# Attention queries of a two-layer model on one core: the rotated parts of four heads in one block of rows, the rest two heads to a block

## The chip, the cores and the metric

The kernel runs on one core of one Trainium2 chip. The metric is the device time of one execution in microseconds; a quoted time is the median of several runs. The profile is of one further execution, and its times are counted from the first instruction of the span.

## The reference, cut to what matters

A model of two layers works on 256 tokens `x` and 256 context tokens `ctx` of width 1024. Layer 0 mixes tokens by an attention of 8 heads beside a long convolution of 512 channels; layer 1 by a gated linear attention; each layer ends in a feed-forward part with a convolution of width 3. All weights are float32. What the change touches is the query of layer 0: 96 numbers for each head, 64 of them plain and 32 rotated (only for the tokens of `x`, not for the context).

```python
q = (rmsnorm(z[..., :256], q_norm_g) @ w_q_b).reshape(lead + (8, 64 + 32))      # for x and for ctx
kv = (rmsnorm(z[..., 256:384], kv_norm_g) @ w_kv_b).reshape(lead + (8, 64 + 64))
q = concatenate([q[..., :64], axial_rope(q[..., 64:], cos, sin)], axis=-1)       # tokens of x only
k, v = keys_values(kv, axial_rope(k_rope, cos, sin))                             # one k_rope for all heads
o = softmax(q k^T / sqrt(96)) v      # 256 queries of x over 512 keys, 256 queries of ctx over their own 256
```

`axial_rope` multiplies a pair of numbers eight places apart with the cosine and the sine of an angle that depends on the token alone, so it is the same for all heads.

## The kernel before

Activations of both sequences lie side by side, 512 tokens along the free dimension. A float32 product is made by `mm3` from two rounded halves of each factor: three matmuls (lines 191 to 193), high by high, high by low, low by high, with the halves made by a copy on ScalarE (line 185 for large weights) and a subtraction on VectorE (line 186).

The stretch around the change is layer 0's mixer. `self.ORDER` (line 1387) lists in which order its pieces are emitted: the heads `("H", 0)` to `("H", 7)`, the long convolutions `c1` and `c2`, the projections `hy` that feed these, the products of attention weights and values `pv`, and six blocks of the modulation weights of layer 0, `mod`, each of which streams 2 MB through two buffers of 512 KB (`mod_row`, line 257). The list is not the order on the engines: a planner with a simulated time line places every emitted instruction on its engine's queue, so that pieces lie interleaved; on the chip each engine then runs its queue in that order.

A head (`mla_head`, line 752) does this. For an even head `head_weights` (line 739) loads the query and key weights of two heads (two DMAs into `hraw`), copies them to `hwh` on ScalarE and subtracts on GpSimd to get `hwl`. Two inner blocks of 128 times three matmuls give the head's 96 query rows for 512 tokens in a PSUM bank `sc`. ScalarE writes them, scaled, to `q` (line 146, by way of `mul_s`). `rope` (line 670) rotates rows 64 to 95 of `q` for the 256 tokens of `x` in four VectorE instructions: a shuffle of partitions (line 674), two products with the table `rope_t` (lines 675 and 676) and a sum (line 677). An even head also projects the keys of two heads and ScalarE copies them to `kt`. Then, four times, a score matmul (line 780), a row maximum on VectorE (line 782), an exponential on ScalarE (line 784), a scaling by the reciprocal of the sum (line 785 and, by way of `mul_s`, 146 or 147), transposes on TensorE (line 789), and a copy out of PSUM (to `ptx` or `ptc`, line 141). There are two `sc` banks and one `tp` bank for this. `mla_first` (line 698) prepares the normalised `zh`, `zl` for all heads, the rotated key rows, and the values.

The long convolution (`long_conv`, line 618) multiplies spectra in lines 650 to 653, on VectorE or on GpSimd; the sums `ua` of lines 639, 640, 655 and 656 are on VectorE.

Of the kernel before, what the change touches and what calls it, by code (L numbers as in the profile page):

```python
# [9 lines left out]
F32 = mybir.dt.float32  # L10
# [14 lines left out]
def constants():  # L25
    c = {}
    c["ident"] = np.eye(128, dtype=np.float32)


    f = np.arange(128) + 0.5  # L30
    tp = np.arange(128)
    mats = []
    for par in range(2):
        ang = 2.0 * np.pi * np.outer(2 * tp + par, f) / 512.0
        mats += [np.cos(ang), np.sin(ang)]
    for par in range(2):
        ang = 2.0 * np.pi * np.outer(f, 2 * tp + par) / 512.0
        mats += [np.cos(ang) / 256.0, np.sin(ang) / 256.0]
    c["dft"] = np.stack(mats, axis=1).reshape(128, 8 * 128).astype(np.float32)

    order = np.concatenate([np.arange(0, 256, 2), np.arange(1, 256, 2)])
    t = np.linspace(0.0, 1.0, 256, dtype=np.float32)[:, None]
    w = (np.float32(2.0 * math.pi) * np.arange(256, dtype=np.float32)[:, None] / np.float32(256)).astype(np.float32)
    fb = np.linspace(1e-4, 15, 16, dtype=np.float32)
    z = np.concatenate([t, np.cos(fb * w), -np.sin(fb * w)], axis=-1).astype(np.float32)
    c["zfeat"] = np.ascontiguousarray(z[order].T)
    lo, hi = math.log(1e-2) / 1.5, math.log(1e-2) / 0.3
    deltas = np.abs(np.linspace(lo, hi, 512, dtype=np.float32))
    win = np.exp(-t * deltas).astype(np.float32)
    c["win"] = np.ascontiguousarray(win.reshape(128, 2, 512)).reshape(128, 1024)  # L50

    rows = SEQ // 64
    row = np.repeat(np.arange(rows), 64).astype(np.float32)
    col = np.tile(np.arange(64), rows).astype(np.float32)
    inv = (np.float32(10000.0) ** (-np.arange(8, dtype=np.float32) / np.float32(8))).astype(np.float32)
    ang = (np.stack([row, col], axis=-1)[..., None] * inv).astype(np.float32)
    rc = np.zeros((32, SEQ), np.float32)
    rs = np.zeros((32, SEQ), np.float32)
    for ax in range(2):
        for half in range(2):  # L60
            for k in range(8):
                i = ax * 16 + half * 8 + k
                rc[i] = np.cos(ang[:, ax, k])
                rs[i] = np.sin(ang[:, ax, k]) * (-1.0 if half == 0 else 1.0)
    c["rope"] = np.concatenate([rc, rs], axis=1)

    i = np.arange(128) % 32
    m = np.zeros((128, 5, 32), np.float32)
    for lv in range(5):
        blk = i >> lv  # L70
        m[:, lv, :] = (blk[:, None] ^ 1) == blk[None, :32]
    c["mask"] = m.reshape(128, 5 * 32)
    return c
# [9 lines left out]
def host(inputs):  # L83

    src = {n: np.ascontiguousarray(inputs[n]) for n in _INS}
    c = constants()
    cols = np.concatenate([np.asarray(inputs[n]).reshape(-1, 128) for n, _ in COLS]).T
    src["cols0"], src["cols1"] = np.ascontiguousarray(cols[:, :NC0]), np.ascontiguousarray(cols[:, NC0:])
    hyp = np.zeros((64, 386), np.float32)
    hyp[:33, 0:256] = c.pop("zfeat")  # L90
    hyp[:33, 256:320] = inputs["hy_w1"][0]
    hyp[:, 320:384] = inputs["hy_w2"][0]
    hyp[:, 384] = inputs["hy_b1"][0]
    hyp[:, 385] = inputs["hy_b2"][0]
    src["hyp"] = hyp
    src.update(c)
    return src

# [2 lines left out]

ENG = dict(pn=(0, 1, 0, 0), pt=(0, 0, 1, 0), q=1, kv=(1, 1), es=1, uh=0, po=1, pr=2, c1=0, zl=0, zh=2, hwh=1, hwl=2, am=(0, 0), sd=(0, 0), ov=1)


class Kern:
# [562 lines left out]
    def rope(self, pool, v):  # L670

        nc = self.nc
        sh = pool.tile([96, 256], F32, tag="rsh", bufs=1, name="rsh")[64:96, :]
        nc.vector.stream_shuffle(sh, v, [i ^ 8 for i in range(32)])
        nc.vector.tensor_tensor(sh, sh, self.rope_t[64:96, 1, :], op=ALU.mult)
        nc.vector.tensor_tensor(v, v, self.rope_t[64:96, 0, :], op=ALU.mult)
        nc.vector.tensor_tensor(v, v, sh, op=ALU.add)

    def tok(self, t):
# [18 lines left out]
    def mla_first(self, mp, pool):  # L698
# [26 lines left out]
        for i in (1, 2):  # L725
            nc.scalar.copy(self.kt[i][64:96, :], kr)

        r = self.load_raw(A["mla_w_kv_b"][0], 0, 1, 0, 1024)
        kvh, kvl = self.split_w(r)
        ov = self.const.tile([128, 2, 4, 512], F32, tag="xo", bufs=1, name="ov")  # L730
# [7 lines left out]

    def head_weights(self, pool, hp):
        nc, A = self.nc, self.A  # L740
        raw = pool.tile([128, 512], F32, tag="hraw", bufs=1, name="hraw")
        nc.sync.dma_start(out=raw[:, :384].rearrange("p (k n) -> p k n", k=2),
                          in_=A["mla_w_q_b"][0][:, hp * 192 : hp * 192 + 192].rearrange("(k p) n -> p k n", p=128))
        nc.sync.dma_start(out=raw[:, 384:].rearrange("p (h c) -> p h c", h=2),
                          in_=A["mla_w_kv_b"][0][:, hp * 256 : hp * 256 + 256].rearrange("p (h c) -> p h c", h=2)[:, :, :64])
        h = pool.tile([128, 512], F32R, tag="hwh", bufs=1, name="hwh")
        l = pool.tile([128, 512], F32R, tag="hwl", bufs=1, name="hwl")
        self.cp(ENG["hwh"], h, raw)
        self.tt(ENG["hwl"]).tensor_tensor(l, raw, h.bitcast(F32), op=ALU.subtract)
        self.hw = (h, l)  # L750

    def mla_head(self, pool, h):
        nc = self.nc
        if h % 2 == 0:
            self.head_weights(pool, h // 2)
        ps = self.bank("sc")
        qbh, qbl = [w[:, :384].rearrange("p (k n) -> p k n", k=2) for w in self.hw]
        kvh, kvl = [w[:, 384:] for w in self.hw]
        for k in range(2):
            c = slice((h % 2) * 96, (h % 2) * 96 + 96)  # L760
            self.mm3(ps[:96, :], (qbh[:, k, c], qbl[:, k, c]), (self.zh[:, k, :], self.zl[:, k, :]), k == 0, k == 1)
        q = pool.tile([96, 512], F32, tag="q", bufs=2, name="q")
        self.mul_s(ENG["q"], q, ps[:96, :], 1.0 / math.sqrt(96.0))
        self.rope(pool, q[64:96, 0:256])
        if h % 2 == 0:

            ps = self.bank("sc")
            self.mm3(ps, (kvh, kvl), (self.zh[:, 2, :], self.zl[:, 2, :]), True, True)
            for i in range(2):
                self.cp(ENG["kv"][i], self.kt[(h + i) % 3][:64, :], ps[64 * i : 64 * i + 64, :])  # L770
        k = self.kt[h % 3]

        sums = pool.tile([128, 4], F32, tag="sums", bufs=2, name="sums")
        ri = pool.tile([128, 4], F32, tag="ri", bufs=2, name="ri")
        ptx = pool.tile([128, 4, 256], F32, tag="ptx", bufs=self.PT, name="ptx")
        ptc = pool.tile([128, 2, 256], F32, tag="ptc", bufs=self.PT, name="ptc")
        for t in range(4):
            c0, n = (0, 512) if t < 2 else (256, 256)
            sc = self.bank("sc")
            nc.tensor.matmul(sc[:, :n], lhsT=q[:, self.tok(t)], rhs=k[:, c0 : c0 + n], start=True, stop=True)  # L780
            nm = pool.tile([128, 1], F32, tag="nm", bufs=4, name="nm")
            nc.vector.tensor_reduce(nm, sc[:, :n], axis=AX.X, op=ALU.max, negate=True)
            p = pool.tile([128, 512], F32, tag="p", bufs=2, name="p")
            nc.scalar.activation(p[:, :n], sc[:, :n], AF.Exp, bias=nm, accum_out=sums[:, t : t + 1])
            nc.vector.reciprocal(ri[:, t : t + 1], sums[:, t : t + 1])
            self.mul_s(ENG["pn"][t], p[:, :n], p[:, :n], ri[:, t : t + 1])
            tp = self.tpps()
            for j in range(n // 128):
                nc.tensor.transpose(tp[:, j * 128 : j * 128 + 128], p[:, j * 128 : j * 128 + 128], self.ident)
            dst = (ptx if t < 2 else ptc)[:, :, (t % 2) * 128 : (t % 2) * 128 + 128]  # L790
            self.cp(ENG["pt"][t], dst, tp[:, :n].rearrange("p (j c) -> p j c", c=128))
        self.pt[h % 2] = (ptx, ptc)
# [44 lines left out]
    def layer0(self):  # L837
        nc, A, tc = self.nc, self.A, self.tc
        with ExitStack() as lc:
# [3 lines left out]
            with self.banks("start", mm=4, tp=2, sc=2):  # L843
# [28 lines left out]
                second = self.anchors  # L872
                m1x = ExitStack()
                m1 = m1x.enter_context(self.pool("mla1", "right"))
                self.rope_t = sp.tile([96, 2, 256], F32, name="rope_t")
                with self.after([self.mod_dma]):
                    nc.sync.dma_start(out=self.rope_t[64:96].rearrange("p a b -> p (a b)"), in_=A["rope"])
                    nc.sync.dma_start(out=self.colt[:, NC0:], in_=A["cols1"])

                nc.gpsimd.tensor_scalar(self.ones, self.ident, 0.0, 1.0, op0=ALU.mult, op1=ALU.add)  # L880
# [540 lines left out]
```

## Time and profile before

| | |
|---|---|
| median of 3 runs | 1170.69 us (1168.97 to 1174.04) |
| the profiled execution | 1175.04 us |
| its span, first to last instruction | 1173.3 us |
| TensorE busy with matmuls | 1137.6 us, 97% |
| VectorE busy | 861.5 us, 73% |
| ScalarE busy | 519.7 us, 44% |
| GpSimd busy | 276.2 us, 24% |
| DMA queue that SyncE issues, share of 16 engines | 42.7% |

A busy TensorE is not a TensorE at its peak: the record of a matmul lasts until its result has left the array, and matmuls overlap, so that the time from one start to the next is the price of one. The share of busy time is a mean over stages with different limits.

### The profile page before, as it was taken

The page shows a single profiled execution, that of the slowest core. Times are in us where ns is not written, and L with a number is a line of the kernel's source. Part 1 is how long each engine was busy: PE and PEld are TensorE (multiplying, and loading weights), DVE is VectorE, ACT ScalarE, POOL GpSimd, SP SyncE. Part 2 cuts the span into 40 slices and gives each one's busy share as a digit, 9 for nine tenths or more (in the row PEclk, how much of TensorE's full clock was granted, in tenths as well). Part 3 has the DMA queues.
Part 4 walks back from the last instruction along what each step waited for, and adds up shares of the span by engine and source line. Part 5 has one row for each costly group of instructions (what it writes and reads, how often), then busy time and mean ns, then how long its engine had stood idle before and what let it go on. Part 6 is the DMA issues. An engine that isn't in the chain of part 4 may idle for free. (4 is left out here: it accounts for less than half of the span.)

```text
span 1173.3 us, 17955 instructions
## 1 busy us (share of the span) xinstructions
PE 1137.6 (97%) x7094; PEld 928.2 (79%) x7094; DVE 861.5 (73%) x1284; ACT 519.7 (44%) x896; POOL 276.2 (24%) x285
## 2 busy tenths in 40 slices
PE   7999988999999999999999999999999999999997
PEld 3587865445888888888888888888888989999985
DVE  4668897786669997989988447565767766877753
ACT  3554333433245444212444236445465456666542
POOL 3110333341011142100111001535657311111110
PEclk9999999998999999999999999999999999999999
DMA  9543221454135552657764223323223354565550
GB/s 338 189 126 90 81 73 43 148 175 154 64 128 196 181 177 93 207 203 246 257 203 138 90 73 108 108 80 102 73 77 105 109 179 140 183 199 173 171 195 36
DMA packets 118055, 167.57 MB, mean 143 GB/s; under 512 B 4658, under 2 KB 74866, under 8 KB 117908
## 3 DMA queue, kind: packets, MB, share of 16 engines
q1 hardware_dynamic: 117540, 165.38, 42.7%
q8 instruction: 56, 0.92, 0.3%
q10 hardware_dynamic: 432, 1.05, 0.2%
q14 instruction: 27, 0.22, 0.1%
HBM read 165.37 MB, written 1.05 MB: 142 GB/s over the span
## 5 line engine op out<-in xcount | busy, mean ns | idle before, releaser
L186 DVE TENSOR_TENSOR lo<-raw,hi 128x1024 fp32r<-128x1024 f32 (+1 forms) x205 | 262.0, 1282 | 151.0 <-ACT hi L185 146.7
L185 ACT CAST hi<-raw 128x1024 fp32r<-128x1024 f32 (+1 forms) x205 | 213.5, 1047 | 325.0 <-PE mm L192 191.8
L192 PE MATMUL mm<-al,hi 128*128 128x512 f32 (+2 forms) x992 | 340.2, 344 | 1.2 <-DVE al L420 1.0
L191 PE MATMUL mm<-ah,hi 128*128 128x512 f32 (+2 forms) x992 | 339.9, 345 | 1.0 <-DVE ah L419 1.0
L193 PE MATMUL mm<-ah,lo 128*128 128x512 f32 (+2 forms) x992 | 340.1, 344 | 0.0
L192 PEld LDWEIGHTS mm<-al,hi 128*128 128x128 f32 x992 | 188.1, 190 | 23.2 <-DVE al L420 1.5
L191 PEld LDWEIGHTS mm<-ah,hi 128*128 128x128 f32 x992 | 187.5, 190 | 23.8 <-DVE ah L419 1.4
L193 PEld LDWEIGHTS mm<-ah,lo 128*128 128x128 f32 x992 | 188.0, 190 | 22.1 <-issue 0.5
L520 POOL TENSOR_TENSOR y<-y 128x512 f32<-128x512 f32 (+1 forms) x44 | 53.5, 1216 | 377.2 <-DVE y L463 319.4
L308 DVE SCALAR_TENSOR_TENSOR macc<-mraw,cs,macc 128x512 f32<-128x512 f32 x140 | 111.1, 804 | 8.7 <-DMA mraw<-in_mod_w_dram 8.0
L191 PE MATMUL mm<-hi,gh 128*128 128x512 f32 x242 | 94.6, 391 | 0.0
L193 PE MATMUL mm<-hi,gl 128*128 128x512 f32 x242 | 94.3, 390 | 0.0
L192 PE MATMUL mm<-lo,gh 128*128 128x512 f32 x242 | 94.2, 390 | 0.0
L191 PE MATMUL mm<-hi,ah 128*128 128x512 f32 (+1 forms) x192 | 74.7, 389 | 0.3 <-DVE modc L285 0.3
L192 PE MATMUL mm<-lo,ah 128*128 128x512 f32 (+1 forms) x192 | 73.7, 384 | 0.0
L193 PE MATMUL mm<-hi,al 128*128 128x512 f32 (+1 forms) x192 | 73.3, 385 | 0.0
L1159 POOL TENSOR_TENSOR gQ<-gQ,gT 128x256 f32<-128x256 f32 x56 | 54.7, 997 | 47.2 <-PE ga L1129 20.4
L1152 DVE TENSOR_TENSOR gK<-gK,gT 128x512 f32<-128x512 f32 (+1 forms) x56 | 50.6, 948 | 13.6 <-ACT gkc L1105 10.4
L193 PEld LDWEIGHTS mm<-hi,gl 128*128 128x128 f32 x242 | 45.4, 188 | 9.5
L192 PEld LDWEIGHTS mm<-lo,gh 128*128 128x128 f32 x242 | 45.4, 188 | 9.3
L191 PEld LDWEIGHTS mm<-hi,gh 128*128 128x128 f32 x242 | 45.4, 188 | 9.2
L459 ACT ACTIVATE y<-mm,col 128x512 f32<-128x512 f32 (+1 forms) x74 | 50.9, 687 | 2.6 <-DVE gl L522 2.6
(301 smaller groups left out, 1779.4 us busy)
## 6 DMA issues: line engine op xcount, KB each, us to landing
mraw<-in_mod_w_dram SPq DMA_DIRECT2D x96, 512.0 KB, 4.7
raw<-in_ffn_w_up_dram SPq DMA_DIRECT2D x44, 1024.0 KB, 5.6
raw<-in_ffn_w_down_dram SPq DMA_DIRECT2D x20, 1024.0 KB, 5.1
raw<-in_hg_w_in_dram SPq DMA_DIRECT2D x20, 1024.0 KB, 5.0
raw<-in_ab_w_in_dram SPq DMA_DIRECT2D x6, 1024.0 KB, 5.2
raw<-in_ab_w_out_dram SPq DMA_DIRECT2D x4, 1024.0 KB, 5.0
raw<-in_hg_w_out_dram SPq DMA_DIRECT2D x4, 1024.0 KB, 5.0
x<-in_x_dram SPq DMA_DIRECT2D x2, 1024.0 KB, 8.3
```

Of the source, the lines that this page charges most:

```text
L185: nc.scalar.copy(hv, v)
L186: nc.vector.tensor_tensor(lv, v, hv.bitcast(F32), op=ALU.subtract)
L191: mm(ps, lhsT=l[0], rhs=r[0], start=start, stop=False)
L192: mm(ps, lhsT=l[0], rhs=r[1], start=False, stop=False)
L193: return mm(ps, lhsT=l[1], rhs=r[0], start=False, stop=stop)
L308: nc.vector.scalar_tensor_tensor(acc[s], w, c, acc[s], op0=ALU.mult, op1=ALU.add)
L459: nc.scalar.activation(y, ps, AF.Identity, scale=w[1], bias=b)
L520: nc.gpsimd.tensor_tensor(ys[1], ys[0], ys[1], op=ALU.mult)
L1152: nc.vector.tensor_tensor(kv, kv, tv, op=ALU.mult)
L1159: nc.gpsimd.tensor_tensor(qv, qv, tq, op=ALU.mult)
```

## The change

The host reorders the query weights: first the 64 plain columns of all heads (512 columns), then the 32 rotated columns of all heads (256). `mla_first` gets a new block that loads the 256 rotated columns (`qraw`, 256 KB), splits them, projects them once, four heads to a block of 128 rows (two blocks, six matmuls each), scales them on ScalarE into `qr` and rotates each block in one call of `rope` over 128 rows; `rope_t` therefore holds the table four times over (256 KB instead of 64 KB). An even head then projects the plain rows of two heads as one block of 128 rows (six matmuls), and for each of the two ScalarE writes 64 scaled rows to `q` and copies the 32 rotated rows from `qr` below them (`cp` with `ENG["qr"]=1` is ScalarE). An odd head projects nothing. There are three `q` buffers instead of two, and `hraw`, `hwh`, `hwl` have 384 columns instead of 512. `self.ORDER` is the same.

```diff
-    c["rope"] = np.concatenate([rc, rs], axis=1)
+    c["rope"] = np.tile(np.concatenate([rc, rs], axis=1), (4, 1))
...
+    wq = np.asarray(inputs["mla_w_q_b"])[0].reshape(256, 8, 96)
+    src["mla_w_q_b"] = np.concatenate([wq[:, :, :64].reshape(256, 512), wq[:, :, 64:].reshape(256, 256)], axis=1)[None]
...
+QB = 3
+ENG = dict(qr=1, pn=(0, 1, 0, 0), ...
...
     def rope(self, pool, v):
-        sh = pool.tile([96, 256], F32, tag="rsh", bufs=1, name="rsh")[64:96, :]
+        ps = slice(0, 128) if v.shape[0] == 128 else slice(64, 96)
+        sh = pool.tile([128, 256], F32, tag="rsh", bufs=1, name="rsh")[ps, :]
         nc.vector.stream_shuffle(sh, v, [i ^ 8 for i in range(32)])
-        nc.vector.tensor_tensor(sh, sh, self.rope_t[64:96, 1, :], op=ALU.mult)
-        nc.vector.tensor_tensor(v, v, self.rope_t[64:96, 0, :], op=ALU.mult)
+        nc.vector.tensor_tensor(sh, sh, self.rope_t[ps, 1, :], op=ALU.mult)
+        nc.vector.tensor_tensor(v, v, self.rope_t[ps, 0, :], op=ALU.mult)
         nc.vector.tensor_tensor(v, v, sh, op=ALU.add)
...
     def mla_first(self, mp, pool):
...
+        raw = pool.tile([128, 2, 256], F32, name="qraw")
+        nc.sync.dma_start(out=raw, in_=A["mla_w_q_b"][0][:, 512:].rearrange("(k p) n -> p k n", p=128))
+        qrh = pool.tile([128, 2, 256], F32R, name="qrh")
+        qrl = pool.tile([128, 2, 256], F32R, name="qrl")
+        nc.scalar.copy(qrh, raw)
+        nc.vector.tensor_tensor(qrl, raw, qrh.bitcast(F32), op=ALU.subtract)
+        self.qr = mp.tile([128, 2, 512], F32, name="qr")
+        for j in range(2):
+            ps = self.bank("sc")
+            for k in range(2):
+                self.mm3(ps, (qrh[:, k, self.tok(j)], qrl[:, k, self.tok(j)]), (self.zh[:, k, :], self.zl[:, k, :]), k == 0, k == 1)
+            nc.scalar.mul(self.qr[:, j, :], ps, 1.0 / math.sqrt(96.0))
+            self.rope(pool, self.qr[:, j, 0:256])
...
     def head_weights(self, pool, hp):
-        raw = pool.tile([128, 512], F32, tag="hraw", bufs=1, name="hraw")
+        raw = pool.tile([128, 384], F32, tag="hraw", bufs=1, name="hraw")
...
     def mla_head(self, pool, h):
         if h % 2 == 0:
             self.head_weights(pool, h // 2)
-        ps = self.bank("sc")
-        for k in range(2):
-            c = slice((h % 2) * 96, (h % 2) * 96 + 96)
-            self.mm3(ps[:96, :], (qbh[:, k, c], qbl[:, k, c]), (self.zh[:, k, :], self.zl[:, k, :]), k == 0, k == 1)
-        q = pool.tile([96, 512], F32, tag="q", bufs=2, name="q")
-        self.mul_s(ENG["q"], q, ps[:96, :], 1.0 / math.sqrt(96.0))
-        self.rope(pool, q[64:96, 0:256])
-        if h % 2 == 0:
+            ps = self.bank("sc")
+            for k in range(2):
+                self.mm3(ps, (qbh[:, k, :], qbl[:, k, :]), (self.zh[:, k, :], self.zl[:, k, :]), k == 0, k == 1)
+            self.q2 = [pool.tile([96, 512], F32, tag="q", bufs=QB, name="q") for _ in range(2)]
+            for i in range(2):
+                self.mul_s(ENG["q"], self.q2[i][:64, :], ps[64 * i : 64 * i + 64, :], 1.0 / math.sqrt(96.0))
+                j = (h + i) % 4
+                self.cp(ENG["qr"], self.q2[i][64:96, :], self.qr[32 * j : 32 * j + 32, (h + i) // 4, :])
             ps = self.bank("sc")
             self.mm3(ps, (kvh, kvl), (self.zh[:, 2, :], self.zl[:, 2, :]), True, True)
...
+        q = self.q2[h % 2]
...
-                self.rope_t = sp.tile([96, 2, 256], F32, name="rope_t")
+                self.rope_t = sp.tile([128, 2, 256], F32, name="rope_t")
```

## Rows read from the trace of the kernel before

**Rows 1.** Busy time of each engine in stretches of the mixer of layer 0, on the core; behind the stretch its length in us, then for each engine its busy us and, in brackets, its instructions, then the granted TensorE clock as a share of full speed, the DMA engines' share and GB/s.

```profile
76.00:108.00 32.00, 30.31 (x143) 23.91 (x142) 24.92 (x42) 15.08 (x23) 2.80 (x2) 1.00 0.36 106
...
150.00:190.00 40.00, 32.77 (x167) 23.22 (x166) 36.64 (x71) 15.54 (x34) 19.21 (x17) 0.91 0.18 60
...
250.00:290.00 40.00, 35.99 (x176) 18.30 (x174) 26.54 (x55) 12.88 (x26) 11.07 (x12) 0.91 0.48 154
76.00:290.00 214.00, 198.94 (x1002) 133.15 (x1001) 168.78 (x314) 82.08 (x159) 59.08 (x51) 0.97 0.35 110
```

**Rows 2.** Who TensorE's matmuls waited for between 76 and 290 us: us in total, times, longest us.

```profile
PE tp L789 <- DVE p L147: 4.3, 2, 3.6
PE sc L780 <- ACT p L784: 3.8, 3, 2.3
PE tp L789 <- DVE ptx L141: 2.7, 1, 2.7
PE sc L780 <- DVE q L677: 1.4, 1, 1.4
```

**Rows 3.** The matmuls of the query and key projections that read `hwh` (their shapes with their counts at the end), and two of them in the time line of TensorE, one behind the other (start us, us).

```profile
L191 PE MATMUL sc<-zh,hwh x20: 387/396/504, 108.8 to 256.9; 128*96 128x512 f32 x16, 128*128 128x512 f32 x4
...
236.21 0.40 PE L192 MATMUL sc<-zl,hwh 128*96 128x512 f32 x1
236.44 0.39 PE L193 MATMUL sc<-zh,hwl 128*96 128x512 f32 x1
```

**Rows 4.** The rotation of the queries on VectorE, 100 to 285 us, by shape: busy us, mean ns of one, idle time before.

```profile
L676 DVE TENSOR_TENSOR q<-q,rope_t 32x256 f32<-32x256 f32 x8 | 8.4, 1048 | 0.0
L675 DVE TENSOR_TENSOR rsh<-rsh,rope_t 32x256 f32<-32x256 f32 x8 | 4.4, 547 | 0.2
L677 DVE TENSOR_TENSOR q<-q,rsh 32x256 f32<-32x256 f32 x8 | 3.8, 469 | 0.3
L674 DVE STREAM_SHUFFLE rsh<-q 32x256 f32<-32x256 f32 x8 | 3.5, 437 | 0.3
```

**Rows 5.** The time line around 176 us, VectorE, GpSimd and TensorE: start us, us, engine, line, in brackets the idle time before and what ended it.

```profile
175.26 0.69 DVE L141 COPY vx<-cv 128x512 f32<-128x512 f32 x1
176.33 2.57 DVE L676 TENSOR_TENSOR q<-q,rope_t 32x256 f32<-32x256 f32 x1
178.93 0.69 DVE L141 COPY ptx<-tp 128x512 f32<-128x512 f32 x1
176.03 2.58 POOL L921 TENSOR_TENSOR vx<-vx,vx 128x1024 f32<-128x1024 f32 x1 [0.46 <-DVE vx L141]
179.67 0.44 PE L789 MATMUL tp<-ident,p 128*128 128x128 f32 x2 [2.68 <-DVE ptx L141]
```

**Rows 6.** The time line around 260 us, VectorE and TensorE, and the same score matmuls of the head before at 244 us.

```profile
259.82 0.44 DVE L674 STREAM_SHUFFLE rsh<-q 32x256 f32<-32x256 f32 x1
260.71 1.11 DVE L675 TENSOR_TENSOR rsh<-rsh,rope_t 32x256 f32<-32x256 f32 x1
261.74 0.94 DVE L676 TENSOR_TENSOR q<-q,rope_t 32x256 f32<-32x256 f32 x1
264.78 0.66 PE L789 MATMUL tp<-ident,p 128*128 128x128 f32 x2 [3.62 <-DVE p L147]
265.55 3.78 PE L780 MATMUL sc<-kt,q 96*128 96x512 f32 x4
...
244.84 1.88 PE L780 MATMUL sc<-kt,q 96*128 96x512 f32 x4
```

**Rows 7.** The time line around 224 us: the scores that waited for the sum of a rotation (VectorE), and the modulation matmuls behind them.

```profile
223.46 0.42 DVE L677 TENSOR_TENSOR q<-q,rsh 32x256 f32<-32x256 f32 x1
223.93 1.98 PE L780 MATMUL sc<-kt,q 96*128 96x512 f32 x4 [1.44 <-DVE q L677]
227.13 1.05 PE L270 MATMUL mm<-mraw,cs 128*32 128x512 f32 x4 [0.23 <-DMA mraw<-in_mod_w_dram]
```

**Rows 8.** The first of six projection matmuls on TensorE at about 187 us, and the last, the sixth.

```profile
186.69 0.63 PE L192 MATMUL mm<-al,hi 128*128 128x512 f32 x1
...
188.82 0.46 PE L191 MATMUL mm<-ah,hi 128*128 128x512 f32 x1
```

**Rows 9.** The front of the stretch: a product over 128 partitions and 256 columns and a split of weights on VectorE, and one issue of SyncE (start us, us).

```profile
102.89 0.42 DVE L652 TENSOR_TENSOR ut<-ut 128x256 f32<-128x256 f32 x1
...
108.28 1.21 DVE L186 TENSOR_TENSOR lo<-raw,hi 128x1024 fp32r<-128x1024 f32 x1
...
66.82 0.34 SPq L169 DMA_DIRECT2D raw<-in_mla_w_kv_b_dram  x1
```

**Rows 10.** Groups on ScalarE between 76 and 285 us that are nearest to its new work: busy us, mean ns of one, idle time before and what ended it.

```profile
L146 ACT ACTIVATE q<-sc 96x512 f32<-96x512 f32 x8 | 4.7, 592 | 9.7 <-PE sc L193 9.7
L141 ACT COPY kt<-sc 64x512 f32<-64x512 f32 x8 | 4.7, 583 | 6.9 <-PE sc L193 6.9
L726 ACT COPY kt<-kt 32x512 f32<-32x512 f32 x2 | 1.1, 613 | 0.0
```

**Rows 11.** DMA issues: the head weights of the queries (KB each, median us to landing), and the modulation loads on SyncE from 206 us (start, us from the first issue to the last), with the times to landing of their 22 issues.

```profile
hraw<-in_mla_w_q_b_dram SPq DMA_DIRECT2D x4, 192.0 KB, 4.4
...
206.04 73.25 SPq L266 DMA_DIRECT2D mraw<-in_mod_w_dram  x22
...
DMA to landing us min/median/max: 3.6/3.7/5.8
```

More of the change, by code (lines that the diff above doesn't have):

```diff
@@ L100 @@
 GSB = 2
-ENG = dict(pn=(0, 1, 0, 0), pt=(0, 0, 1, 0), q=1, kv=(1, 1), es=1, uh=0, po=1, pr=2, c1=0, zl=0, zh=2, hwh=1, hwl=2, am=(0, 0), sd=(0, 0), ov=1)
+QB = 3
+ENG = dict(qr=1, pn=(0, 1, 0, 0), pt=(0, 0, 1, 0), q=1, kv=(1, 1), es=1, uh=0, po=1, pr=2, c1=0, zl=0, zh=2, hwh=1, hwl=2, am=(0, 0), sd=(0, 0), ov=1)
 class Kern:
@@ L740, in head_weights @@
         nc, A = self.nc, self.A
-        raw = pool.tile([128, 512], F32, tag="hraw", bufs=1, name="hraw")
-        nc.sync.dma_start(out=raw[:, :384].rearrange("p (k n) -> p k n", k=2),
-                          in_=A["mla_w_q_b"][0][:, hp * 192 : hp * 192 + 192].rearrange("(k p) n -> p k n", p=128))
-        nc.sync.dma_start(out=raw[:, 384:].rearrange("p (h c) -> p h c", h=2),
+        raw = pool.tile([128, 384], F32, tag="hraw", bufs=1, name="hraw")
+        nc.sync.dma_start(out=raw[:, :256].rearrange("p (k n) -> p k n", k=2),
+                          in_=A["mla_w_q_b"][0][:, hp * 128 : hp * 128 + 128].rearrange("(k p) n -> p k n", p=128))
+        nc.sync.dma_start(out=raw[:, 256:].rearrange("p (h c) -> p h c", h=2),
                           in_=A["mla_w_kv_b"][0][:, hp * 256 : hp * 256 + 256].rearrange("p (h c) -> p h c", h=2)[:, :, :64])
-        h = pool.tile([128, 512], F32R, tag="hwh", bufs=1, name="hwh")
-        l = pool.tile([128, 512], F32R, tag="hwl", bufs=1, name="hwl")
+        h = pool.tile([128, 384], F32R, tag="hwh", bufs=1, name="hwh")
+        l = pool.tile([128, 384], F32R, tag="hwl", bufs=1, name="hwl")
         self.cp(ENG["hwh"], h, raw)
@@ L755, in mla_head @@
             self.head_weights(pool, h // 2)
-        ps = self.bank("sc")
-        qbh, qbl = [w[:, :384].rearrange("p (k n) -> p k n", k=2) for w in self.hw]
-        kvh, kvl = [w[:, 384:] for w in self.hw]
-        for k in range(2):
-            c = slice((h % 2) * 96, (h % 2) * 96 + 96)
-            self.mm3(ps[:96, :], (qbh[:, k, c], qbl[:, k, c]), (self.zh[:, k, :], self.zl[:, k, :]), k == 0, k == 1)
-        q = pool.tile([96, 512], F32, tag="q", bufs=2, name="q")
-        self.mul_s(ENG["q"], q, ps[:96, :], 1.0 / math.sqrt(96.0))
-        self.rope(pool, q[64:96, 0:256])
-        if h % 2 == 0:
+            qbh, qbl = [w[:, :256].rearrange("p (k n) -> p k n", k=2) for w in self.hw]
+            kvh, kvl = [w[:, 256:] for w in self.hw]
+            ps = self.bank("sc")
[6 more added lines that the diff above has]
+                self.cp(ENG["qr"], self.q2[i][64:96, :], self.qr[32 * j : 32 * j + 32, (h + i) // 4, :])
             ps = self.bank("sc")
@@ L874, in layer0 @@
                 m1 = m1x.enter_context(self.pool("mla1", "right"))
-                self.rope_t = sp.tile([96, 2, 256], F32, name="rope_t")
+                self.rope_t = sp.tile([128, 2, 256], F32, name="rope_t")
                 with self.after([self.mod_dma]):
-                    nc.sync.dma_start(out=self.rope_t[64:96].rearrange("p a b -> p (a b)"), in_=A["rope"])
+                    nc.sync.dma_start(out=self.rope_t.rearrange("p a b -> p (a b)"), in_=A["rope"])
                     nc.sync.dma_start(out=self.colt[:, NC0:], in_=A["cols1"])
```

## The prediction

> **What bounds the kernel now.** The page of the profile has TensorE busy for 97% of the span, so the first question is whether the stretch that the change touches is full as well. The stretches of the mixer answer it [rows 1]: between 76 and 290 us TensorE is busy 199 of 214 us, and of the 15 us that are missing 7.2 lie between 150 and 190 us and 4.0 between 250 and 290 us. In the first of these VectorE is busy 36.6 of 40 us. Both have a granted clock of 0.91: part of the time TensorE ran at 1.2 GHz and not at 2.4. The next view is who TensorE waited for [rows 2]: 4.3 us for a scaled row on VectorE, 3.8 us for exponentials, 2.7 us for a copy out of PSUM on VectorE, 1.4 us for the sum of a rotation. Three of these four are VectorE's queue. So the stretch has two limits: where long matmul blocks lie it is TensorE's work, and between the scores and the products of a head it is a chain in which VectorE comes last. The change takes work from both, and puts some on ScalarE, which is busy 82 of the 214 us.
>
> **TensorE's work.** The query matmuls are 16 for each of three kinds, 48 [rows 3]. After, there are 4 pairs by 6, and 2 blocks by 6 in front: 36. One costs the time to the next start, 0.23 us, not its recorded 0.39 us [rows 3]; a block of 128 weight columns has the same 512 columns to stream, and I take the same. 12 fewer give -2.8 us where TensorE is the limit and 0 where it waits anyway; I take -2.8. The Trainium skill, "TensorE: Matmul & The Clock Gate", section "Back-to-back issue gap", gives about 131 ns as the sustained spacing of matmuls of 512 columns. By it the term would be 12 x 0.131 = -1.6 us; the trace disagrees, with 0.23 us, and the trace decides.
>
> **VectorE's work.** Eight rotations take 8.4 + 4.4 + 3.8 + 3.5 = 20.1 us [rows 4], 2.5 us for a head. Two remain beside the keys' own. Their price over 128 rows is no row of before; the nearest, a product over 128 partitions and 256 columns, took 0.42 us [rows 9], near the 0.47 us that a sum over 32 rows took in the mean [rows 4]; the dearest of the old products took 2.57 us [rows 5]. Time goes by columns, not by rows, so four instructions at 0.42 are 1.7 us for each call. The new split is one subtraction over 512 columns, about half of the 1.21 us of the 1024-column one [rows 9]. So VectorE loses some 16 us in the heads and gains 4.0 us in front of them. What that is worth is read wait by wait.
>
> At 176 us a product of the rotation ran 2.57 us beside a GpSimd product of 2.58 us, where the eight of its kind took 1.05 us in the mean [rows 4, 5]. The copy to `ptx` stood behind it, and TensorE waited 2.68 us for that copy [rows 5]. Without the rotation the copy follows the one that ended at 175.95 us. Next in line is that copy's own 0.69 us, before the wait began; I take the whole wait, -2.7 us, between 0 and that.
>
> At 260 us three instructions of the rotation, 0.44 + 1.11 + 0.94 = 2.5 us, lie ahead of the scaled row for which TensorE waited 3.62 us [rows 6]. What is late next is the same scaled row, behind two small modulation operations. I take -2.5 us, between 0 and -3.6.
>
> At 224 us the scores waited 1.44 us for the sum of the rotation itself. But the second modulation block behind them already waited 0.23 us for its DMA [rows 7], and that landing does not move with the scores. I take half, -0.7, between 0 and -1.4. The 3.8 us behind exponentials [rows 2] hang on row maxima that stand behind convolution products; I take nothing of it, though up to 2.3 could go.
>
> **The clock.** After both long waits TensorE fell to 1.2 GHz. Five matmuls from 186.69 us on are (188.82 - 186.69) / 5 = 0.43 us apart and not 0.23, 1.0 us lost [rows 8], and four scores took 3.78 us where the head before took 1.88, 1.9 us lost [rows 6]. If the waits go, some of the fall goes with them: half, -1.5 us, between 0 and -2.9.
>
> **What it adds.** ScalarE gets eight copies from `qr` to `q` and two scalings of a whole block, and one cast. The nearest rows are 0.59 us for 96 or 64 rows and 0.61 us for 32 rows [rows 10]: price goes by columns, and a quarter of the rows is no cheaper. 11 x 0.6 = 6.6 us more on an engine that is idle 132 of 214 us [rows 1]. For a pair ScalarE now has four writes of queries and two of keys in a run, 3.5 us, where an even head had three, 1.8 us, and an odd one a single write. If exponentials of the head before stand behind it, TensorE waits for its score banks: between 0 and 4 x 1.8 = 7.1 us. I take +1.0, near the free end, because a query written early by two heads has no rotation to wait for and its place in the queue is loose.
>
> In front, 4.0 us of VectorE work join the chain that feeds the third convolution projection, while the first head's own 1.7 us leave it, so its splits (one at 108.28 us, [rows 9]) come up to 2.3 us later. What hides it is the matmuls of the weights split before: TensorE is busy 30.3 of the 32 us up to 108 [rows 1]. If that cover is gone, 2.3 us are lost; I take +1.0.
>
> The query weights are as many bytes as before: 4 loads of 192 KB [rows 11] become 4 of 128 KB and one of 256 KB. The extra load is one issue more on SyncE's queue, emitted ahead of that of the value weights at 66.8 us [rows 9], and with some 4.4 us to landing [rows 11] it is there long before the first query matmul at 108.8 us [rows 3]. The table's 192 KB more pass when no load bounds TensorE. The smaller weight splits on GpSimd and the third `q` buffer only loosen. All of this at 0.
>
> **The sum.** -2.8 - 2.7 - 2.5 - 0.7 - 1.5 + 1.0 + 1.0 = -8.2 us. All pieces are placed anew by the planner, though, and the place where one wait ended is where the next one in line is found; I take back a quarter of the 7.4 us of waits and clock, +1.9. That leaves -6.3 us. The profiled execution took 1175.04 us, so it would take 1168.7; the median of the runs is 4.35 us below that execution, so the median becomes 1164.4, 0.5% faster. About 0.5%, 5.9 us, is also what a measurement of this kernel can tell from no change: a gain counts as one below 1164.8. My own range for this case is 1158 to 1169.
>
> **Rivals.** *The waits go whole.* TensorE's 2.8, the whole of 2.7, 3.6, 1.4 and 2.3 us of waits and 2.9 us of clock, and nothing new: -15.7 us, 1155. For it speaks that VectorE is the last releaser in most waits; against it, that convolution work stands in the same queue.
>
> *The modulation loads set the pace from 206 us on.* 22 loads of 512 KB pass two buffers in 73.25 us, each takes 3.7 us to land [rows 11] and its matmuls about 1.05 us [rows 7]. At two buffers, 11 rounds of 4.75 us, 52 us, is the least. So there are 21 us of room in all, but a single round has little, as at 227 us. Then gains behind 206 us are lost. Ahead of it 30 matmuls become 30 (12 in front and 3 pairs), -2.7 and the first clock loss of 1.0 remain, and the additions of +2.0: about -1.7 us, 1169: no difference.
>
> *ScalarE's run takes the place of the rotation.* If the run of six writes stands ahead of the exponentials in each of the four pairs, TensorE loses 7.1 us, and since the same scores and transposes then wait for ScalarE, none of the waits above is won. With 2.3 us in front and -2.8 of work: +6.6 us, 1177. It decides against the change once the run costs more than some 2.1 us for a pair, with the waits not won. For it: exponentials are what TensorE waits for already, 3.8 us [rows 2]. Against it: ScalarE's idle time. The Trainium skill, "PSUM — Partial Sum Buffer", section "Engine vs sequencer instructions", says that ScalarE's queue is strictly first in, first out. By that rule an exponential cannot pass the run, which is what this rival needs; no run here shows it yet for the new order.
>
> **How the numbers follow.** The forecast has 0.55, with 0.33 of it beyond 0.5% and 0.22 inside; the waits going whole 0.09; the modulation loads 0.15, within 0.5%; ScalarE's run 0.21, of which 0.18 is slower by over 0.5% and 0.03 within. Faster 0.42, same 0.40, slower 0.18. The range goes from a microsecond short of the waits going whole, 1156, to two short of ScalarE's full price, 1175; some 0.06 lies below and 0.14 above.
>
> **What would show it.** In the profile after: 36 query matmuls; two rotations over 128 rows at 0.42 us an instruction; VectorE's busy time between 76 us and the end of the mixer down by 10 to 16 us and ScalarE's up by about 6; no wait for a rotation, and the waits for `ptx` and the scaled row shorter; a granted clock nearer to 1 in both stretches; the first `ab_w_out` matmuls some 6 us earlier, and the distance from there to the end unchanged. It is wrong if TensorE's waits for exponentials grow past 3.8 us, if the modulation matmuls wait for DMA by more than a microsecond or two, or if the part behind the mixer moves.

## The result, and the profile after

The changed kernel takes 1164.55 us, the median of 14 runs (1160.93 to 1171.09); the kernel before took 1170.99 us beside it (14 runs, 1168.97 to 1176.14). The ratio is 0.9944, with a 95% interval of 0.9928 to 0.9961: 6.4 us faster. The forecast was 1164.4.

The two profiled executions differ by more, 1173.3 against 1162.5 us of span, and the difference has to be divided first. Both kernels run the same matmul `mm<-hi,ah` at the start of the stretch (the first block of `ab_w_in`) and at its end (the first block of `ab_w_out`). I call the time between these two the mixer. Before, it goes from 45.48 to 285.50 us, after from 40.86 to 273.40 us. So 4.6 us of the 10.8 lie ahead of it, 7.5 in it, and behind it the changed kernel is 1.3 us longer. The 4.6 us belong to that one execution of the kernel before: eight matmuls at 13.9 us took 7.17 us there and 3.67 us after, by lines that the change does not touch, and a later kernel with the order of the one before (below) came to its mixer at 41.22 us, as all the other profiled executions did between 40.8 and 41.3 us. -7.5 + 1.3 is -6.2, near the 6.4 of the medians.

The whole mixer of the kernel before, with the columns of [rows 1]:

```profile
45.48:285.50 240.02, 224.96 (x1148) 155.46 (x1146) 183.47 (x348) 95.98 (x193) 62.99 (x55) 0.97 0.33 103
```

The whole mixer of the changed kernel, and two stretches of it, same columns:

```profile
40.86:273.40 232.54, 219.30 (x1135) 153.86 (x1133) 173.24 (x324) 105.07 (x207) 59.21 (x55) 0.97 0.37 117
...
150.00:190.00 40.00, 34.72 (x180) 25.93 (x181) 33.02 (x61) 17.49 (x38) 16.23 (x14) 0.91 0.19 59
250.00:290.00 40.00, 34.53 (x161) 21.17 (x160) 22.71 (x43) 10.62 (x20) 3.83 (x6) 0.87 0.54 184
```

VectorE lost 10.2 us of work and ScalarE gained 9.1. TensorE is busy 5.7 us less, and its idle time fell only from 15.1 to 13.2 us. Who it waited for after, answering to [rows 2]:

```profile
PE sc L800 <- ACT p L804: 4.4, 4, 3.5
PE mm L274 <- DMA mraw<-in_mod_w_dram: 3.4, 3, 1.8
PE mm L195 <- DVE vx L467: 1.2, 1, 1.2
PE cv L666 <- DVE ua L659: 1.1, 2, 0.7
```

The scaled row, `ptx` and the sum of the rotation, 8.4 us in [rows 2], are gone. In their place stand modulation loads (3.4 us, 0.2 before) and convolution work. All of the 7.5 us lie behind the first modulation matmuls: these start 157.6 us behind the mixer's first matmul in both kernels (with 779 matmul records ahead of them after, 757 before), and from there to the mixer's end it is 82.4 us before and 74.9 after. The tail of the mixer in TensorE's time line shows the new waits, with nothing else between the last two bursts of modulation matmuls:

```profile
263.38 1.08 PE L823 MATMUL po<-ptc,ov 128*64 128x256 f32 x6 [0.52 <-DVE ptc L145]
266.27 1.92 PE L274 MATMUL mm<-mraw,cs 128*32 128x512 f32 x4 [1.81 <-DMA mraw<-in_mod_w_dram]
269.34 1.92 PE L274 MATMUL mm<-mraw,cs 128*32 128x512 f32 x4 [1.15 <-DMA mraw<-in_mod_w_dram]
272.00 1.12 PE L285 MATMUL mm<-ident,modrow 128*128 128x128 f32 x4 [0.74 <-ACT modrow L278]
273.40 0.80 PE L195 MATMUL mm<-hi,ah 128*128 128x512 f32 x1 [0.28 <-DVE modc L289]
274.00 0.63 PE L196 MATMUL mm<-lo,ah 128*128 128x512 f32 x1
274.42 0.63 PE L197 MATMUL mm<-hi,al 128*128 128x512 f32 x1
274.85 0.63 PE L195 MATMUL mm<-hi,ah 128*128 128x512 f32 x1
```

From 266.2 us, behind a wait of 1.81 us, TensorE runs at 1.2 GHz for 10.2 us: the same four matmuls take 1.92 us that took 1.05 [rows 7], and the first `ab_w_out` matmuls, which follow at once, still stand 0.43 us apart (274.42 to 274.85 us). That is where most of the 1.3 us behind the mixer went.

The new work itself in the groups of the changed kernel (busy us, mean ns of one, idle time before): a product and the sum of the rotation on VectorE, the new writes on ScalarE, and one of the three kinds of query matmuls, plain with the keys' four, and rotated:

```profile
L681 DVE TENSOR_TENSOR qr<-qr,rope_t 128x256 f32<-128x256 f32 x2 | 0.8, 420 | 0.0
L682 DVE TENSOR_TENSOR qr<-qr,rsh 128x256 f32<-128x256 f32 x2 | 0.8, 420 | 0.0
...
L145 ACT COPY q<-qr 32x512 f32<-32x512 f32 x8 | 4.9, 616 | 0.1
L150 ACT ACTIVATE q<-sc 64x512 f32<-64x512 f32 x8 | 4.7, 592 | 7.2 <-PE sc L197 7.1
...
L195 PE MATMUL sc<-zh,hwh 128*128 128x512 f32 x12 | 5.3, 438 | 0.0
...
L195 PE MATMUL sc<-zh,qrh 128*128 128x512 f32 x4 | 1.5, 416 | 0.0
```

### The profile page after: what moved, and what is told of

It is laid out like the page before. It is cut to its first block, busy times and chain, and to the rows that moved or that the text cites. A ratio compares the mean times of both kernels' runs of the same rounds, so it can differ in the third digit from the quotient of the medians.

```text
span 1162.5 us, 17910 instructions
## 1 busy us (share of the span) xinstructions
PE 1128.2 (97%) x7082; PEld 926.5 (80%) x7082; DVE 844.5 (73%) x1255; ACT 524.9 (45%) x907; POOL 274.8 (24%) x285
## 3 DMA queue, kind: packets, MB, share of 16 engines
q10 hardware_dynamic: 432, 1.05, 0.2%
HBM read 165.57 MB, written 1.05 MB: 143 GB/s over the span
## 5 line engine op out<-in xcount | busy, mean ns | idle before, releaser
L196 PEld LDWEIGHTS mm<-al,hi 128*128 128x128 f32 x992 | 188.0, 190 | 23.2 <-DVE al L424 1.5
L524 POOL TENSOR_TENSOR y<-y 128x512 f32<-128x512 f32 (+1 forms) x44 | 56.5, 1284 | 374.5 <-DVE y L467 313.2
L1172 DVE TENSOR_TENSOR gK<-gK,gT 128x512 f32<-128x512 f32 (+1 forms) x56 | 50.3, 942 | 14.1 <-ACT gkc L1125 10.4
```

The costliest lines, as they stand in the source:

```text
L196: mm(ps, lhsT=l[0], rhs=r[1], start=False, stop=False)
L524: nc.gpsimd.tensor_tensor(ys[1], ys[0], ys[1], op=ALU.mult)
L1172: nc.vector.tensor_tensor(kv, kv, tv, op=ALU.mult)
```

## The experiments

The theory was that TensorE's work (12 matmuls) and VectorE's relief at three waits make the gain. The rival was that the stream of modulation loads, or the new order that the planner lays whenever a cost changes, decides how much of it is kept. This table collects what the experiments below gave. The median comes from all runs of a kernel; the mixer's length, TensorE's waits for modulation loads in it, and the time of the modulation matmuls on TensorE come from one profiled execution each, with the falls of the clock that this execution happened to have.

| kernel | median us | mixer us | waits for loads us | modulation matmuls us |
|---|---|---|---|---|
| before | 1170.99 | 240.0 | 0.2 | 25.5 |
| before, three `q` buffers | 1172.18 | 240.4 | 0 | 25.8 |
| before, rotation on 32 columns | 1173.97 | 242.0 | 7.7 | 24.1 |
| before, no rotation | 1184.34 | 249.9 | 10.4 | 26.8 |
| after | 1164.55 | 232.5 | 3.4 | 26.0 |
| after, rotated head by head | 1169.48 | 235.5 | 10.3 | 23.0 |
| after, 12 more matmuls | 1174.11 | 241.1 | 7.9 | 25.1 |
| after, modulation block earlier | 1165.39 | 231.2 | 3.1 | 23.2 |
| after, loads in halves | 1168.12 | 233.9 | 0 | 31.7 |
| after, copies on VectorE | 1167.15 | 230.2 | 4.6 | 23.5 |
| before, half of the loads | 1169.72 | 237.5 | 0 | 13.8 |
| before, no rotation, half of the loads | 1166.76 | 233.2 | 0.5 | 17.6 |
| after, 12 more, half of the loads | 1169.56 | 232.9 | 0 | 14.5 |
| after, half of the loads | 1165.51 | 228.3 | 0.7 | 14.7 |

**One rotation for each head, all else as after.**

```diff
-            self.rope(pool, self.qr[:, j, 0:256])
...
+                self.rope(pool, self.q2[i][64:96, 0:256])
```

> The changed kernel, but the rotated parts are projected once and copied to each head unrotated, and each head is rotated on its own again: eight rotations over 32 rows instead of two over 128. It keeps the 12 matmuls that the change saves and gives VectorE its 16 us back. Theory (VectorE's relief is the larger part, the matmuls 2.8 us of it): 1168 to 1171 us, and waits for a rotation are back in the profile. Rival (the saved matmuls and the new order of the queues give the gain): 1164 to 1166 us.

Measured: 1169.48 us, ratio 0.9991 (0.9976 to 1.0007) to before. The number is the theory's, the mechanism is not: no wait for a rotation, for `ptx` or for a scaled row came back among TensorE's largest. What came is waits for loads.

```profile
PE mm L274 <- DMA mraw<-in_mod_w_dram: 10.3, 10, 4.2
```

**Twelve more query matmuls, all else as after** (three more for each pair, whose sums are overwritten).

```diff
+            self.mm3(ps, (qbh[:, 0, :], qbl[:, 0, :]), (self.zh[:, 0, :], self.zl[:, 0, :]), True, True)
```

> The changed kernel with three matmuls more for each pair of heads, whose sums are overwritten: the 12 matmuls that the change saves are put back, VectorE keeps its relief. Theory: at most 2.8 us over the changed kernel (1164.5), so 1165 to 1167.5 us, less where TensorE waits anyway. Rival (the matmuls are the gain): 1169 to 1171 us.

Measured: 1174.11 us, 1.0037 (1.0016 to 1.0058), 9.6 us above the changed kernel and not 2.8: above the theory and above the rival. Twelve matmuls do not last that long: in the mixer TensorE is busy only 2.4 us more (221.7 against 219.3), but idle 6.2 us more (19.4 against 13.2). The order changed with them, and waits for loads rose from 3.4 to 7.9 us.

**No rotation of the queries, all else as before** (part of the computation is left out).

```diff
-        self.rope(pool, q[64:96, 0:256])
```

> The kernel before without the rotation of its queries (left out: the queries of x are not rotated), so VectorE has 20 us less to do and nothing else changes. Theory: most of the gain without the change's matmuls and without ScalarE's copies, 1162 to 1166 us. Rival (the waits turn to another releaser, VectorE's work was not what bound): 1169 to 1171 us.

Measured: 1184.34 us, 1.0118 (1.0091 to 1.0145). Neither the theory nor its rival has this: with 20 us of VectorE's work taken away the kernel is 13 us slower. TensorE's longest wait in it:

```profile
PE mm L270 <- DMA mraw<-in_mod_w_dram: 10.4, 5, 5.7
```

And the end of its mixer, by engines:

```profile
250.00:290.00 40.00, 29.31 (x144) 12.40 (x143) 19.93 (x39) 11.81 (x23) 10.70 (x12) 0.83 0.69 225
```

TensorE is busy 29.3 of these 40 us (34.5 in the changed kernel), with the DMA engines at 0.69 of their time, and it runs at 1.2 GHz for 17.1 us from 276.4 us on.

**Three `q` buffers, all else as before** (`bufs=2` becomes `bufs=3` in the tile `q`).

> The kernel before with three buffers for q instead of two, and nothing else: the planner places the queues anew from a program with the same work. It measures what a new order alone is worth, and the third buffer. Theory: within 2 us of the kernel before, 1169 to 1173 us. Rival (gain and loss of this size come from the order of the queues alone): off by 4 us or more to either side.

Measured: 1172.18 us, 1.0013 (0.9996 to 1.0029). Every engine's instructions stand in the same order as before. The buffer alone is worth nothing. Since it is the same order, the run does not tell what a new order alone is worth; but its mixer of 240.4 us beside 240.0 gives a first idea, from one pair, of how far two profiled mixers of one order lie apart.

**Half of the modulation loads left out, after and before.** This asks whether the stream is what the changed kernel ends on.

```diff
         for h in range(4):
-            raw = self.modp.tile([128, 2, 512], F32, tag="mraw", bufs=self.MB, name="mraw")
-            self.mod_dma = nc.sync.dma_start(out=raw, in_=W[h * 256 : h * 256 + 256, ...
+            if self.MB != 2 or h % 2 == 0:
+                raw = self.modp.tile([128, 2, 512], F32, tag="mraw", bufs=self.MB, name="mraw")
+                self.mod_dma = nc.sync.dma_start(out=raw, in_=W[h * 256 : h * 256 + 256, ...
```

> The changed kernel, with every second load of the modulation weights in the mixer left out (the matmuls take the half that is there twice, so that part of the output is not computed; all instructions of TensorE stay). Theory: the changed kernel's front is now bound from 199 us to its end by the stream of modulation loads (10.8 us of waits of TensorE and its weight loads for them in the profile, 3.4 of them of the matmuls alone, and 10.2 us at half clock at 264 to 276 us around the last two). Then 1157 to 1161. Rival: the waits for loads only fill time in which TensorE would have waited for VectorE or ScalarE anyway. Then 1163 to 1166.

> The kernel before, with the same loads left out (that part of the output is not computed). Theory: before, VectorE and not the stream of modulation loads set the end of the front (2.3 us of TensorE's waits were for them), so 1169 to 1171.5. Rival: the stream bounds both kernels, and then this falls as far as the other one, to 1164 to 1168.

Measured: 1165.51 us after (0.9936, 0.9913 to 0.9959) and 1169.72 before (0.9979, 0.9959 to 0.9999). In time the theory has it for the kernel before, and the rival for the changed kernel: nothing is won. In the profile its mixer is 4.2 us shorter (228.3 against 232.5), but the part behind it is 5.2 us longer (894.3 against 889.1). The stretch from 964 to 968 us in this kernel, columns as above:

```profile
964.00:968.00 4.00, 4.00 (x20) 4.00 (x20) 1.68 (x3) 1.16 (x4) 0.00 (x0) 0.50 0.49 165
```

And in the changed kernel with all loads:

```profile
964.00:968.00 4.00, 3.58 (x30) 3.19 (x29) 2.44 (x4) 3.35 (x9) 0.00 (x0) 1.00 0.03 9
```

From 956.4 us on TensorE ran at 1.2 GHz for 13.7 us here, and not at all in the changed kernel's execution. The runs point the same way: the seven of this kernel have a mean granted clock of 0.981 to 0.984 and took 1162.9 to 1167.3 us, and the three of the changed kernel at 0.983 to 0.984 took 1170.8 to 1171.1. So the median does not tell what the mixer won.

The experiment also takes away more than waits. The modulation matmuls use 32 columns of the array each, four groups of them side by side, and one load feeds two groups. A matmul leaves two records (96 for the 48 modulation matmuls of the mixer). With half of the loads, eight records need one load and run at once (TensorE's time line of this kernel):

```profile
237.77 1.07 PE L275 MATMUL mm<-mraw,cs 128*32 128x512 f32 x8
```

In the kernels with all loads most bursts are of four records, which take 1.05 us [rows 7]. So the matmuls' own time fell from 26.0 to 14.7 us, and the 4.2 us of the mixer are not the price of waiting for loads alone.

**Loads of 256 KB through four buffers, all else as after.**

```diff
+        if self.MB == 2:
+            for h in range(8):
+                raw = self.modp.tile([128, 512], F32, tag="mraw", bufs=4, name="mraw")
+                self.mod_dma = nc.sync.dma_start(out=raw, in_=W[h * 128 : h * 128 + 128, c0 : c0 + 512]).ins
+                ops += [(self.cs[:, h, :], raw)]
```

> The changed kernel, with the modulation weights of the mixer loaded in pieces of 256 KB through four buffers in place of 512 KB through two: the same bytes in the same space, twice the DMA instructions on SyncE's queue. Theory (the two buffers bound the stream: a buffer is free only when its last matmul has run, and the next piece lands 3.6 us after its issue): smaller pieces free and land earlier, 1160 to 1163. Rival: the stream is bound by when it may start (199.6 us, behind the load of ab_w_out at 193.6 us on SyncE's queue) or is no bound: 1164 to 1166, or up to 1168 for the added issues.

Measured: 1168.12 us, 0.9965 (0.9948 to 0.9981). TensorE's waits for loads are gone, and yet it is no faster than the changed kernel: the median is 3.6 us higher, its mixer 1.3 us longer, and the two intervals just overlap. A piece now feeds one column group, and a burst for it lasts as long as one for two or four (time line of this kernel):

```profile
239.78 1.05 PE L279 MATMUL mm<-mraw,cs 128*32 128x512 f32 x2
```

The modulation matmuls take 31.7 us in place of 26.0, which eats what the waits gave: TensorE's idle time in the mixer falls from 13.2 to 8.1 us, and its busy time grows from 219.3 to 225.7.

**The first modulation block earlier, all else as after.**

```diff
-                      ("H", 5), ("c2", 1, 0, 0), ("pv", 2, True), ("c2", 1, 1, 0), ("c2", 0, 0, 1), ("mod", 0, 2, 0), ("c2", 0, 1, 0),
+                      ("mod", 0, 2, 0), ("H", 5), ("c2", 1, 0, 0), ("pv", 2, True), ("c2", 1, 1, 0), ("c2", 0, 0, 1), ("c2", 0, 1, 0),
```

> The changed kernel, with its first modulation block of the mixer ahead of the rows of the fifth head pair's step in the written order of the front, not behind the second convolution pieces. Theory (the time at which the stream of modulation loads starts sets the end of the front): the stream starts some us earlier and the time falls by about as much, 1159 to 1163. Rival: the stream is not the bound, or the block's matmuls only move ahead of work that VectorE waits for: 1164 to 1168.

Measured: 1165.39 us, 0.9938 (0.9917 to 0.9960): the same as the changed kernel. The stream did start earlier, its first burst of matmuls at 194.3 us and not at 198.5, but the last came at 269.4 us against 269.3, with 3.1 us of waits for loads against 3.4. When the stream starts is not what sets the end.

**Half of the loads in the two kernels that went against the theory.** Does the stream explain why they were slow? Both leave the loads out as above.

> The kernel before without the rotation of the queries (not computed), and with every second load of the modulation weights in the mixer left out as well (the matmuls take the half that is there twice). Theory: without rotation it took 1184.3 because its order made TensorE wait 10.4 us for modulation loads and run at half clock for 17 us behind them; without half of the loads these go, and it takes 1166 to 1172. Rival: the order costs the time in other places: 1177 or more.

> The changed kernel with twelve more query matmuls (their sums are overwritten), and with every second load of the modulation weights in the mixer left out (the matmuls take the half that is there twice). Theory: the twelve matmuls cost 9.6 us in place of 2.8 because the new order waits 7.9 us for modulation loads; without half of the loads they cost what they take, so 1166 to 1169 (the changed kernel with half of the loads took 1165.5). Rival: 1172 to 1176, the order costs it elsewhere.

Measured: 1166.76 us without the rotation (0.9955, 0.9940 to 0.9970), 17.6 us below the same kernel with all loads; and 1169.56 us with twelve more matmuls (0.9978, 0.9965 to 0.9990), 4.5 us below. The first is as the theory had it. The second is half a microsecond above its bound, and below the rival. Halving the loads takes 16.7 and 8.2 us out of these two mixers, and 2.5 and 4.2 out of those of before and after, while the modulation matmuls' own time falls by 9 to 12 us in all four. So the stream is most of what made these orders slow.

With it halved, the four mixers seem to add up: 237.5 before, 233.2 without the rotation, 232.9 with the changed kernel's rotation and 48 matmuls, 228.3 with both, which would be 4.3 to 4.6 us for VectorE's relief and 4.6 for the twelve matmuls. But these are no prices of the two parts. The granted clock in the four mixers is 0.94, 0.97, 0.98 and 0.96. Between the last two the 4.6 us are idle time, 20.0 against 14.4 us: TensorE is busy 1.0 us less in the kernel that has twelve matmuls more. And from the first to the third TensorE's busy time falls by 7.1 us, while its idle time grows by 2.5. What each part is worth by itself is not shown.

**A shorter rotation, all else as before** (32 of its 256 columns; the others stay unrotated).

```diff
+        w = slice(0, 32)
+        nc.vector.stream_shuffle(sh[:, w], v[:, w], [i ^ 8 for i in range(32)])
...
```

> The kernel before, with each rotation worked on 32 of its 256 columns (the other columns stay unrotated): all its instructions stay, VectorE's time for them falls by about 9 us over the front, and the planner, which sees shorter instructions, lays a new order. Theory (the gain of the change is VectorE's relief at the places where TensorE waits for it): 1163 to 1167. Rival (what the new order does with the stream of modulation loads weighs more than the relief, as in the kernel before without any rotation, 1184): 1170 to 1184.

Measured: 1173.97 us, 1.0037 (1.0019 to 1.0055). The theory fails here too. The planner laid a new order, and in it TensorE waited 7.7 us for loads and ran at 1.2 GHz for 10.2 us from 277.1 us on. Its longest wait:

```profile
PE mm L270 <- DMA mraw<-in_mod_w_dram: 7.7, 4, 5.4
```

**The copies on VectorE, all else as after** (`ENG` with `qr=0`).

> The changed kernel, with the copies of the rotated rows into the heads' tiles on VectorE in place of ScalarE: 8 copies, 616 ns each on ScalarE, some 0.3 to 0.45 us each on VectorE, which is where the front's waits come from. Theory (VectorE's time is what the front pays for, ScalarE's is hidden): 1165 to 1168. Rival (ScalarE's 4.9 us of copies lie on the path): 1160 to 1163.

Measured: 1167.15 us, 0.9952 (0.9935 to 0.9970). The median is where the theory had it, but the interval overlaps that of the changed kernel, and the profile says the contrary: the mixer is 2.3 us shorter (230.2) and the part behind 5.7 us longer, with 13.7 us at 1.2 GHz from 958.8 us on. At the same mean granted clock of 0.993 the two kernels agree, with 1161.1 us here and 1160.9 to 1161.4 in the changed kernel. Which engine should copy stays open.

## Why the prediction was right, point by point

The prediction gives two ranges, 1158 to 1169 as its own and 1156 to 1175 from the rivals; 1164.55 lies in both. The total was right to 0.2 us, and that is in part luck: the waits and TensorE's work gave more than the sum has for them, the clock gave nothing, and more came back. All three signs that the prediction names for being wrong appeared, each by a little: waits for exponentials of 4.4 us, above 3.8; waits for modulation loads of 3.4 us; and the part behind the mixer moved by 1.3 us. A granted clock nearer to 1 in both stretches did not come (0.91 and 0.87, after 0.91 and 0.91 [rows 1]).

**TensorE's work, -2.8.** 36 query matmuls, as forecast: of each kind there are 12 with the keys' four among them, and 4 rotated, where there were 20 [rows 3]. What their records add to TensorE's busy time, each from the end of the one before it, falls by 3.0 us. So 2.8 was the right size. TensorE's whole busy time fell by 5.7 us, though; the other 2.7 are in no term.

**The waits at VectorE, -2.7, -2.5 and -0.7.** All three places went whole and not in part: 2.7, 4.3 and 1.4 us of [rows 2] are no longer in the list, 8.4 us against 5.9 forecast. The working says that VectorE loses some 16 us in the heads and gains 4.0 in front; by its own rows all 20.1 leave the heads, and 16 is the net. Measured in the mixer it is 10.2, mostly because other work fell into the stretch: 21 splits over 1024 columns where there were 17, 25.8 us against 21.3. A call of the rotation took four instructions of 0.42 to 0.45 us over 128 rows, as forecast, and none was stretched as the one of 2.57 us in [rows 5].

**Given back, +1.9.** This is the term that was too small. TensorE's idle time fell by 1.8 us where 8.4 of waits went, so 6.6 us of others came: 3.2 for modulation loads (3.4 against 0.2), the rest for convolution work (1.2 for `vx`, 1.1 for `ua`), exponentials (0.6 more) and smaller ones. The loads are the forecast's second rival, with its sign of more than a microsecond or two. It did not decide: its price of 3.4 us stands against 8.4 us of waits that went, and its premise, that gains behind 206 us are lost, did not hold. From the first of its matmul bursts to the last the stream took 79.5 us before and 70.8 after, so it had room. But in four kernels with other orders it took 7.7 to 10.4 us, and most or all of the gain with it. Had the planner laid such an order for this change, the rival's 1169 might have been the better forecast.

**The clock, -1.5.** Nothing: 13.7 us of the mixer at 1.2 GHz before, 14.0 after. The falls at 185 and 264 us of before [rows 6, 8] went with their waits. But one of 3.4 us at 168.5, where TensorE had waited 2.3 us for an exponential, became one of 6.8 us at 163.8, where it waits 3.5 us at the same point of the work, and one of 10.2 us came at 266.2.

**ScalarE, +1.0.** The price of one copy was right (616 ns against 0.6 us). Its work in the mixer grew by 9.1 us where 6.6 was forecast; 6.0 of it are the writes of queries (4.9 + 4.7 + 1.1 against 4.7 in [rows 10]). The waits for exponentials went from 3.8 to 4.4 us; a run of writes ahead of them in all four pairs, which the third rival needs, would have been 7.1. The longest wait, 3.5 us, was not ScalarE's doing: ScalarE had been idle for 5.36 us, until a row maximum on VectorE that stood behind convolution products (VectorE, ScalarE and TensorE in the changed kernel):

```profile
159.97 1.64 DVE L655 TENSOR_TENSOR ua<-ua,kspec 128x512 f32<-128x512 f32 x1
161.54 1.48 DVE L656 TENSOR_TENSOR ut<-ut 128x256 f32<-128x256 f32 x1
162.94 0.68 DVE L802 TENSOR_REDUCE nm<-sc 128x1 f32<-128x512 f32 x1
163.65 0.69 ACT L804 ACTIVATE p<-sc,nm 128x512 f32<-128x512 f32 x1 [5.36 <-DVE nm L802]
164.48 1.22 PE L800 MATMUL sc<-kt,q 96*128 96x256 f32 x2 [3.51 <-ACT p L804]
```

So VectorE is still the last link there, as the prediction's first paragraph has it. The Trainium skill, "PSUM — Partial Sum Buffer", section "Engine vs sequencer instructions", has ScalarE's queue first in, first out. No run here contradicts that. The rival failed because the run of writes did not make TensorE wait; its limit of 2.1 us for a pair was wrong as well, since by its own sum (5.9 + 2.8 - 2.3) / 4 is 1.6 us.

**The front, +1.0.** No wait shows this cost. In the 32 us that begin 30.5 us behind the mixer's first matmul (76 to 108 us before, 71.38 to 103.38 after), TensorE is busy 30.31 us [rows 1] and 30.57 us.

**The part behind.** Forecast as unchanged, it is 1.3 us longer in the profile, by the end of the fall of the clock that the last loads brought.

In one line, for the mixer: waits gone -8.4, new waits +6.6, TensorE's busy time -5.7 (3.0 of it the query matmuls, 1.7 the transposes of attention rows, which are as many as before and only stand in another order), together -7.5; and +1.3 behind it.

What stays open: whether the changed kernel's own order is good by its work or by chance, and so what the twelve matmuls and VectorE's relief are worth each. Every edit that changed a cost was planned anew, so no run holds the order and changes the work. An order laid down by hand was not tried.

## What to carry to other kernels

When a planner lays the order, a gain is that of work and order together: here taking work away made the kernel 13 us slower, and the same relief with twelve more matmuls brought nothing. Cost an edit against the resource that comes next in line (here two buffers of modulation weights) and not only against the waits that it removes. To see a gain of some microseconds, measure the stretch between two fixed instructions of the profile beside the median of the whole.

## What the runs showed of the hardware

**A burst of narrow matmuls costs the same for one, two or four column groups.** With 32 weight columns each, two records on one group took 1.05 us, four on two groups 1.05, eight on four groups 1.07. The Trainium skill, "TensorEngine Tiling (Array Packing)", section "Key Properties", says that different tiles can run loads of weights and matmuls in parallel; the traces agree, with those three times. So what a load brings should fill all four groups. Dividing a load's 512 columns over two more groups might do that for the 24 loads of this mixer with all of its bytes; it was not tried.

**The clock falls at a place that the edit does not touch.** In seven of the fourteen profiled executions, TensorE ran at 1.2 GHz for 10.2 to 13.7 us from a moment between 956 and 980 us on; the part behind the mixer took 891 to 895 us in these and 887 to 890 us in the others. It came in kernels of either sort, and TensorE's waits around it were no longer than in the changed kernel, where it did not come (the longest 0.8 us in both, with half of the loads and with all). The changed kernel's fourteen runs spread with the clock too: 1160.9 to 1161.4 us where the mean granted clock was 0.993, 1170.8 to 1171.1 where it was 0.983 to 0.984. One such fall lowers that mean by 0.004 to 0.006 (half of 10.2 to 13.7 us in 1162.5), so by this estimate it is about half of the difference. What brings it in one execution and not in the next was not found.
